# A hybrid decoder trunk: the mixing stage's small inverse, its spreads and its order of work

## The chip, the cores and the metric

The kernel runs on one core of one Trainium2 chip. The metric is the device time of one execution in microseconds (us). The engines are PE (TensorE, the matrix products), DVE (VectorE), ACT (ScalarE), POOL (GpSimd) and SP (SyncE, here only a queue that issues DMA transfers). PEld is the loading of weights into PE, beside its products. A DMA stands in the queue of the engine that issues it, and a queue is worked off in its order.

## What is computed

Two layers, each of a gated feed-forward block, a mixing block and a second feed-forward block, on 512 tokens of width 1024, all in float32. The change touches the mixing block and the normalization ahead of each block. In the mixing block the normalized input is projected to 2560 columns, which three heads of different kind share: sliding-window attention (8 query heads, 2 key heads, window 128, with sinks), RWKV-7 time mixing (4 heads of 64) and a short gated convolution. The outputs are joined and projected back to 1024.

```python
def rms_norm(x, gain):
    y = xf * lax.rsqrt(jnp.mean(xf * xf, axis=-1, keepdims=True) + EPS)
    return y * gain
def sliding_window_sink_attention(qkv, q_gain, k_gain, sinks):
    ...
    scores = einsum('bnqhgd,bnkhd->bnhgqk', qb, kb) * HEAD_DIM ** -0.5
    probs = softmax(concatenate([where(mask, scores, -inf), sink], -1))[..., :-1]
    out = einsum('bnhgqk,bnkhd->bnqhgd', probs, vb)
def rwkv7_time_mix(p, mu, ...):
    p = p + mu * (token_shift(p) - p)
    r, k, v, wd, ad, gd = split(p, ...)
    ...
    def step(S, inp):
        s_kk = einsum('bhvk,bhk->bhv', S, kk_t)
        S = S * w_t - s_kk * (kk_t * a_t) + v_t * k_t
        return S, einsum('bhvk,bhk->bhv', S, r_t)
    y = group_norm(scan(step)) ; y = (y + sum(r * k * r_k) * v) * g
```

## The kernel before

Activations lie with features on the 128 partitions and the 512 tokens along the free axis. A product of a weight tile and an activation tile in float32 is made of three products (`mm3`, L113 to 120): the high part of the weight with the high and the low part of the activation, and the low part of the weight with the high part. They stand in the profile as L118, L119 and L120. The split of a weight tile is a cast on ACT (wH, L130) and a subtraction on DVE (wL, L132), and `load_w` (L277 to 286) brings the raw tile (wraw, two buffers) through SP's queue.

`mix()` (from L577) holds the mixing block. The large projection is a row of 20 tiles of 24 products each, written by the generator `products()` (L668) in the order decay/iclr, k (two), key (kt), value (vr), query (four), r (two), v (two), gate (gd) and convolution (six). Two PSUM banks named "mm" take the tiles in turn, so a tile's first product waits until the tile two before it has left its bank: for r, v and gd by `shifted` (L620), a copy on ACT (L622) and two or more steps on DVE (L627). Beside it three generators run, each in small steps:

- `inverse()` (L800) inverts 64x64 unit triangular blocks (32 of them, two q halves). It takes LT, the masked products of beta and a in B, and moves its 16x16 diagonal blocks through DRAM: two transfers into dl (L809) and sixteen small ones into G (L815). On DVE it then runs 15 elimination steps of two instructions each (elim L822, inv L823; step 7 is followed by a pause). One transfer into di (L828) and sixteen into C (L831) bring the result back, and T and its transpose TT are made on DVE (L837, L838). All 35 transfers of a layer are issued by SP.
- `rwkv()` (L843) makes roots of sums of squares (`roots`, L644) and spreads each over the 64 partitions of its head by products with the identity (`spread_heads`, L660: ps_kk for kk, ps_ks for kt, ps_v for the group norm), then the pairs of chunks (ps_c on PE, masked into B and K on DVE, L924), the bonus (ps_bo), four sets of block transposes (vN with ps_vN, AX with ps_ta, beN, kaN), the corrections of T and TT in two levels (ps_x, X L1012, ps_t, L1023), and the state.
- `attention()` (L1110) works through four blocks of 128 queries: scores (ps_sc, Sc), the softmax (mx, es, the exponentials on ACT in L1150, the division L1178 to 1180), transposes of the probabilities (ps_pt on PE, pmc and pmp on DVE L1167), products with V (ps_av) and a copy of the result into qr (L1190).

Which step stands where is set by a loop with a clock, at the end of `mix()`. Each step of a generator yields two numbers: how far it moves the clock, and how long its successor must wait, which a table `PACE` scales per generator; a group of three large products moves the clock by `STEP`, 0.65. When a step is due, it is written into the program behind the large products so far, and its first matmul is held there (`pe`, L632).

```python
n = min(live, key=ready_.get, default=None)
if n and (ready_[n] <= clock or stuck or not more):
    clock = max(clock, ready_[n])
    lead[0] = latest["large"]
    step = next(live[n], None)
    ...
    clock += step[0]
    ready_[n] = clock + step[1] * PACE[n]
```

Within one engine the order of instructions is fixed when the program is built. The norm ahead of every block spreads the reciprocal root of each half of the tokens over the partitions by two 128x128 products with the identity (`spread`, L258, ps_rstd L264).

Of the kernel before, what the change touches and what calls it, by code (L numbers as in the profile page):

```python
# [17 lines left out]
P = 128  # L18
# [16 lines left out]
PACE = {"rwkv": 1.15, "att": 1.05, "LT": 1.0}  # L35
# [24 lines left out]
def trunk_kernel(ctx, tc, ins, out, layers=L, phases=("ffn1", "mix", "ffn2")):  # L60
# [177 lines left out]
    def norm(l, g, ish, isc, ss):  # L238
# [21 lines left out]
        def spread(sl):  # L260

            r, pt = rstd[sl.start], psum([P, T // 2], "ps_rstd", "r0" if sl.start else "x")
            for b in range(2):
                mm(pt[:, b * P : (b + 1) * P], r[:, b : b + 1].to_broadcast([P, P]), cst("ident"), start=True, stop=True)  # L264
            rstd[sl.start] = pt
# [311 lines left out]
    def mix(l, hn, ss, mp, then, ready):  # L577
# [66 lines left out]
        def roots(srcs, name, bias, scale, low=None):  # L644
# [13 lines left out]
            return r  # L658

        def spread_heads(r, pts):  # L660

            for i, pt in enumerate(pts):
                for b in range(NB):
                    for g in range(2):
                        pe(pt[rows[g], b * P : (b + 1) * P], r[:, i, b, g : g + 1].to_broadcast([P, CH]), cst("ident"), start=True, stop=True)
            return pts

        def products():  # L668
# [108 lines left out]
            done.add("in")  # L777
            while "ya" not in done:
                yield "stuck"
# [4 lines left out]
            for i in range(KD - 2):  # L784
                w = load_w(wo1[l, i, :, :6], 6)
                pt = psmm()
                for k in (4, 5, 0, 1, 2, 3):
# [12 lines left out]
        def inverse():  # L800
# [6 lines left out]
            for q in range(2):  # L807
                dl = dram.tile([P, 2 * NB, CH], F32, name="dl", tag=f"dl{q}", bufs=2)
                nc.sync.dma_start(dl, LT[q].rearrange("p e b t -> p (e b) t"))  # L809
                for c in range(2):  # L810
                    for m in range(NM):
# [3 lines left out]
                        nc.sync.dma_start(G[n : n + 2 * NB], src.rearrange("r n t -> n r t"))  # L815
# [12 lines left out]
            nc.sync.dma_start(di.rearrange("q m n t u -> (q m n) t u"), V_)  # L828
            for q in range(2):
                for m in range(2 * NM):  # L830
                    nc.sync.dma_start(C_[q][m * BASE : (m + 1) * BASE], di[q, m].rearrange("n t u -> t n u"))  # L831
# [11 lines left out]
        def rwkv():  # L843
# [47 lines left out]
            yield 1.0, 6.5  # L891
# [33 lines left out]

            pairs(be, B_, 0, 1)
# [7 lines left out]
            yield 0, 3.2  # L934
            while "r" not in done:
# [9 lines left out]
            yield 1.4, 2.6  # L945
            while "v" not in done:
                yield 0, STEP
# [6 lines left out]
            AX = [U(q, "AX", [P, 2, NB, 2, CH]) for q in range(2)]  # L954
            vN, beN, kaN = ([blocks(S(q, n)) for q in range(2)] for n in ("vN", "beN", "kaN"))
            qs = both()
            pv, pt = banks("ps_vN"), banks("ps_ta")
            for q in qs:
                for b in range(NB):
                    pe(blocks(pv[q])[:, b], v_[q][:, b * P : (b + 1) * P], cst("cen"), start=True, stop=True)  # L960
                turn_(blocks(pt[q]), AR[q][:, 0].rearrange("p c t -> p (c t)"))
            for q in qs:
                nc.scalar.copy(vN[q], blocks(pv[q]))
                for e in range(2):
                    nc.scalar.copy(AX[q][:, e, :, 0], blocks(pt[q])[:, :, rows[e]])
            yield 2.6, 3.4
            qs = both()
            pv, pt = banks("ps_beN"), banks("ps_kaN")
            for q in qs:
                turn_(blocks(pv[q]), be[q])  # L970
                turn_(blocks(pt[q]), ka[q])
            for q in qs:
                nc.scalar.copy(beN[q], blocks(pv[q]))
                nc.scalar.copy(kaN[q], blocks(pt[q]))
            yield 1.8, 3.2

            corners = [(b, e, c) for b in range(NB) for e, c in ((1, 1), (1, 0), (0, 1), (0, 0))]

            def quarters(name, n=1, w=CH):
                return [[psum([P, n, NB, w], name, R[q]) for _ in range(2)] for q in range(2)]  # L980

            def gathered(pts, j):

                return [(slice(0, P), 0, pts[0][:, j])] + [(rows[c], 1, pts[1][rows[1 - c], j]) for c in range(2)]

# [12 lines left out]
            T_, TT = got["T"], got["TT"]  # L998
            X = [S(q, "X", (P, 2, NB, CH)) for q in range(2)]

            def each(q, pts, j, lhs, rhs):
                for b, e, c in corners:
# [492 lines left out]
```

## Time and profile before

| | |
|---|---|
| median of three runs | 1843.88 us (1842.59 to 1846.69) |
| profiled execution | 1847.01 us, of which the span is 1845.0 |
| mixing stages | about 380 to 600 and 1285 to 1505 us |
| DMA, mean over the span | 167 GB/s |

The span runs from the first to the last recorded instruction of the profiled execution; some 2 us lie around it. Rows of a timeline give the start in us from the span's start, the duration, the engine, the line, the operation and output<-inputs, with the idle time before it and what ended it in brackets. A row "PE ps_sc L634 <- ACT qr L1190: 2.3, 1, 2.3" of the waits says that PE, at a product into ps_sc, stood idle for 2.3 us until ACT's step on qr was done. x4 counts neighbouring instructions in one row; a float32 product of the small kind takes several passes and stands as several instructions.

### The profile page before, as it was taken

The numbers are of one execution on the slowest core, as the hardware profiler recorded it, in microseconds if no ns is written. First come the engines' busy times: TensorE is split into PE (matmuls) and PEld (weight loads), VectorE is DVE, ScalarE is ACT, GpSimd is POOL, SyncE is SP. The second block draws the span as 40 slices with busy tenths as digits, with TensorE's granted clock in tenths as the row PEclk, the third lists the DMA queues.
The fourth block names the chain that finished last, engine by engine and source line by source line (L and its number), as shares of the span: only waits on it lengthen the run. The fifth ranks groups of instructions, "written<-read, shape, count | busy, mean of one in ns | idle before, by whom it ended". The sixth has DMA issues, their size and how long they took to land.

```text
span 1845.0 us, 34043 instructions
## 1 busy us (share of the span) xinstructions
PE 1797.7 (97%) x13996; PEld 1634.6 (89%) x13996; DVE 1354.7 (73%) x2185; ACT 837.6 (45%) x1284; POOL 130.7 (7%) x208
## 2 busy tenths in 40 slices
PE   8999999999999999999999999999999999999999
PEld 6889899987778899899999988999867788999998
DVE  6687687876776787678878786878677677874872
ACT  4443255363533554145446524544544445532551
POOL 0101110100000001110100011110000000110000
PEclk8999999999999999999999999999999999999999
DMA  7667876623112476886737688773321125774742
GB/s 312 225 179 237 287 200 198 217 75 99 34 45 91 121 206 188 280 206 198 250 110 197 172 275 233 194 227 123 109 76 39 59 78 158 215 221 139 203 140 69
DMA packets 104284, 308.37 MB, mean 167 GB/s; under 512 B 23360, under 2 KB 24384, under 8 KB 103104
## 3 DMA queue, kind: packets, MB, share of 16 engines
q1 hardware_dynamic: 75904, 203.42, 33.2%
q0 software_dynamic: 28224, 102.77, 22.2%
q8 instruction: 110, 1.80, 0.4%
q14 instruction: 46, 0.38, 0.1%
HBM read 302.74 MB, written 3.41 MB: 166 GB/s over the span
## 4 chain that ended last, share of the span: by engine, by line
PE 73%; DVE 11%; DMA 6%; issue 4%; ACT 4%; POOL 1%; SPq 1%; DVEq 0%; ACTq 0%; POOLq 0%
PE ps_mm L118 11%; PE ps_mm L119 11%; PE ps_mm L120 11%; PE ps_d L414 6%; PE ps_d L416 6%; PE ps_d L415 6%; PE ps_f L415 3%; PE ps_f L416 3%; PE ps_f L414 3%; DVE wL L132 2%; DMA wada<-in_wadaT 2%; PE ps_g L416 2%; ACT wH L130 2%; PE ps_g L415 2%; PE ps_g L414 2%
## 5 line engine op out<-in xcount | busy, mean ns | idle before, releaser
L130 ACT CAST wH<-wraw 128x1024 fp32r<-128x1024 f32 (+2 forms) x292 | 265.8, 917 | 471.6 <-PE ps_mm L119 218.4
L132 DVE TENSOR_TENSOR wL<-wraw,wH 128x1024 fp32r<-128x1024 f32 (+2 forms) x292 | 308.5, 1061 | 123.7 <-ACT wH L130 122.2
L120 PE MATMUL ps_mm<-actH,wL 128*128 128x512 f32 (+1 forms) x784 | 280.7, 358 | 1.3 <-DVE wL L132 1.3
L118 PE MATMUL ps_mm<-actH,wH 128*128 128x512 f32 (+1 forms) x784 | 281.0, 358 | 0.0
L119 PE MATMUL ps_mm<-actL,wH 128*128 128x512 f32 (+1 forms) x784 | 280.5, 358 | 0.0
L118 PE MATMUL ps_mm<-hnH,wH 128*128 128x512 f32 (+1 forms) x760 | 268.1, 360 | 11.0 <-DVE mx L1142 3.3
L119 PE MATMUL ps_mm<-hnL,wH 128*128 128x512 f32 (+1 forms) x760 | 267.1, 353 | 1.1 <-DVE hnL L273 0.9
L120 PE MATMUL ps_mm<-hnH,wL 128*128 128x512 f32 (+1 forms) x760 | 264.9, 351 | 0.6 <-DVE wL L132 0.6
L414 PE MATMUL ps_d<-comH,wH 128*128 128x256 f32 x816 | 226.3, 277 | 0.0
L416 PE MATMUL ps_d<-comH,wL 128*128 128x256 f32 x816 | 226.0, 277 | 0.0
L415 PE MATMUL ps_d<-comL,wH 128*128 128x256 f32 x816 | 225.9, 277 | 0.0
L188 DVE SCALAR_TENSOR_TENSOR wada<-wada,crep 128x1024 f32<-128x1024 f32 x140 | 167.7, 1221 | 47.5 <-DMA wada<-in_wadaT 47.2
L132 DVE TENSOR_TENSOR wL<-sum,wH 128x1024 fp32r<-128x1024 f32 x102 | 125.0, 1225 | 73.6 <-ACT wH L130 73.5
L118 PEld LDWEIGHTS ps_mm<-hnH,wH 128*128 128x128 f32 x760 | 143.5, 192 | 39.0 <-issue 13.8
L120 PEld LDWEIGHTS ps_mm<-actH,wL 128*128 128x128 f32 x784 | 148.7, 190 | 18.9 <-DVE wL L132 2.1
L119 PEld LDWEIGHTS ps_mm<-actL,wH 128*128 128x128 f32 x784 | 148.7, 190 | 16.7
L118 PEld LDWEIGHTS ps_mm<-actH,wH 128*128 128x128 f32 x784 | 148.7, 190 | 16.5
L119 PEld LDWEIGHTS ps_mm<-hnL,wH 128*128 128x128 f32 x760 | 145.9, 192 | 17.4 <-DVE hnL L273 2.2
L120 PEld LDWEIGHTS ps_mm<-hnH,wL 128*128 128x128 f32 x760 | 145.9, 192 | 15.9 <-DVE wL L132 1.4
L414 PEld LDWEIGHTS ps_d<-comH,wH 128*128 128x128 f32 x816 | 158.2, 194 | 0.6 <-ACT s L440 0.6
L415 PEld LDWEIGHTS ps_d<-comL,wH 128*128 128x128 f32 x816 | 158.2, 194 | 0.0
L416 PEld LDWEIGHTS ps_d<-comH,wL 128*128 128x128 f32 x816 | 158.1, 194 | 0.0
(358 smaller groups left out, 3753.0 us busy)
## 6 DMA issues: line engine op xcount, KB each, us to landing
wada<-in_wadaT POOLq DMA_DIRECT2D x128, 512.0 KB, 4.8
wraw<-in_wmi SPq DMA_DIRECT2D x40, 512.0 KB
wraw<-in_w2p SPq DMA_DIRECT2D x36, 512.0 KB
wraw<-in_w1p SPq DMA_DIRECT2D x32, 512.0 KB
wraw<-in_w1o SPq DMA_DIRECT2D x32, 384.0 KB
wraw<-in_w2o SPq DMA_DIRECT2D x32, 384.0 KB
wraw<-in_w1i SPq DMA_DIRECT2D x20, 512.0 KB
wraw<-in_w1o SPq DMA_DIRECT2D x32, 320.0 KB
```

The source lines that it names most:

```text
L118: mm(acc, wH, xH, start=start, stop=False)
L119: mm(acc, wH, xL, start=False, stop=False)
L120: latest["large"] = mm(acc, wL, xH, start=False, stop=stop)
L130: nc.scalar.copy(hi, src)
L132: return nc.vector.tensor_sub(lo, src, hi.bitcast(F32))
L188: stt(w, w, 1.0, crep, ALU.mult, ALU.mult, accum_out=out_)
L414: mm(acc, wH, xH, start=start and i + k == 0, stop=False, skip_group_check=True)
L415: mm(acc, wH, xL, start=False, stop=False, skip_group_check=True)
L416: mm(acc, wL, xH, start=False, stop=k == 3, skip_group_check=True)
```

## The change

1. The clock's table: PACE of rwkv from 1.15 to 1.25, of attention from 1.05 to 1.0, and several yields.
2. The norm's spread is made by transposes instead of products with the identity.
3. `roots` writes each root twice 64 columns wide on ACT into a tile "wide", and `spread_heads` makes one 128x128 transpose of it where two products of 64 columns stood.
4. The inverse's 35 transfers per layer are issued by POOL instead of SP.
5. The transposes of beta (beN) and a (ta) stand ahead of the wait for r; those of key (kaN) come with vN.
6. The corrections of T become a generator of their own, which may begin while v is awaited if T is there.
7. Two output tiles begin with their products of the convolution's halves (k = 4, 5) before attention's last step is awaited.

```diff
-PACE = {"rwkv": 1.15, "att": 1.05, "LT": 1.0}
+PACE = {"rwkv": 1.25, "att": 1.0, "LT": 1.0}
 def spread(sl):
-    mm(pt[:, b * P : (b + 1) * P], r[:, b : b + 1].to_broadcast([P, P]), cst("ident"), start=True, stop=True)
+    mm(pt[:, b * P : (b + 1) * P], r[:, b : b + 1].to_broadcast([P, P]), cst("ident"), start=True, stop=True, is_transpose=True)
 def roots(srcs, name, bias, scale, low=None):
-    return r
+    wide = U(0, "wide", [P, n, NB, 2, CH])
+    for i in range(n):
+        nc.scalar.copy(wide[:, i], r[:, i].unsqueeze(3).to_broadcast([P, NB, 2, CH]))
+    return wide
 def spread_heads(r, pts):
-    for g in range(2):
-        pe(pt[rows[g], b * P : (b + 1) * P], r[:, i, b, g : g + 1].to_broadcast([P, CH]), cst("ident"), start=True, stop=True)
+    pe(pt[:, b * P : (b + 1) * P], r[:, i, b].rearrange("p g z -> p (g z)"), cst("ident"), start=True, stop=True, is_transpose=True)
 def products():
+    begun = []
+    for i in range(2):
+        begun.append((load_w(wo1[l, i, :, :6], 6), psmm()))
+        for k in (4, 5):
+            mm3(begun[i][1], begun[i][0], k, xs[k], ALL, k == 4, False)
+            yield
     while "ya" not in done:
         yield "stuck"
...
 def inverse():
-    nc.sync.dma_start(dl, LT[q].rearrange("p e b t -> p (e b) t"))
+    nc.gpsimd.dma_start(dl, LT[q].rearrange("p e b t -> p (e b) t"))
...
-    nc.sync.dma_start(G[n : n + 2 * NB], src.rearrange("r n t -> n r t"))
+    nc.gpsimd.dma_start(G[n : n + 2 * NB], src.rearrange("r n t -> n r t"))
...
-    nc.sync.dma_start(di.rearrange("q m n t u -> (q m n) t u"), V_)
+    nc.gpsimd.dma_start(di.rearrange("q m n t u -> (q m n) t u"), V_)
...
-    nc.sync.dma_start(C_[q][m * BASE : (m + 1) * BASE], di[q, m].rearrange("n t u -> t n u"))
+    nc.gpsimd.dma_start(C_[q][m * BASE : (m + 1) * BASE], di[q, m].rearrange("n t u -> t n u"))
 def rwkv():
     rn = roots(sq, "rn", None, None, 1e-24)
-    yield 1.0, 6.5
+    yield 1.7, 7.2
...
+    pv, pt = banks("ps_beN"), banks("ps_ta")
+    for q in qs:
+        turn_(blocks(pv[q]), be[q])
+        turn_(blocks(pt[q]), AR[q][:, 0].rearrange("p c t -> p (c t)"))
+    for q in qs:
+        nc.scalar.copy(beN[q], blocks(pv[q]))
+        for e in range(2):
+            nc.scalar.copy(AX[q][:, e, :, 0], blocks(pt[q])[:, :, rows[e]])
+    yield 1.8, 3.4
     while "r" not in done:
         yield 0, STEP
...
+    inv = invert()
     while "v" not in done:
-        yield 0, STEP
+        yield next(inv) if "T" in done else (0, STEP)
...
     while "T" not in done:
         yield 0, STEP
-    for lev in range(2):
...
+    yield from inv
...
-    yield 2.8, 0.4
+    yield 3.4, 1.0
     pv = spread_heads(rs, banks("ps_v"))
 def attention():
-    yield 0.4, 2.0
+    yield 0.4, 3.2
     po = psum([P, 4, P], "ps_av")
...
-    yield 1.9, 1.2
+    yield 1.9, 1.6
```

The rows below are the order of instructions of one engine in layer 1, with the line, the operation, output<-inputs and the shape; numbers behind a name tell buffers apart, and x2 counts neighbours. Lines of the changed kernel lie about ten further down in `inverse()` and fourteen in `attention()`.

First the transfers. SP before, from the weight loads ahead of the inverse (wraw<-in_wmi is a tile of the projection's weights, in_wmo of the output projection's; dl, G, di and C are the inverse's):

```order
L1092 DMA gw<-in_gw 128x256
L284 DMA wraw<-in_wmi 128x1024 x4
L809 DMA dl<-B_4188 1024x1x64
L809 DMA dl<-B_4189 1024x1x64
L815 DMA G<-dl 8x16x16 x16
L284 DMA wraw<-in_wmi 128x1024 x4
L828 DMA di<-inv 128x256
L284 DMA wraw<-in_wmi 128x1024
L831 DMA C<-di 16x8x16 x16
L284 DMA wraw<-in_wmi 128x1024 x2
```

SP in the changed kernel at the same place (gw is the gate's small weight), and POOL there, from attention's first clearing of its scores:

```order
L611 DMA lw<-in_lora 128x256
L284 DMA wraw<-in_wmi 128x1024 x4
L1106 DMA gw<-in_gw 128x256
L284 DMA wraw<-in_wmi 128x1024 x11
L284 DMA wraw<-in_wmo 128x768 x6
```

```order
L1134 MEMSET Sc 128x512 x2
L826 MEMSET inv 128x256
L827 MEMSET inv 128x16
L819 DMA dl<-B_4190 1024x1x64
L819 DMA dl<-B_4191 1024x1x64
L825 DMA G<-dl 8x16x16 x16
L838 DMA di<-inv 128x256
L841 DMA C<-di 16x8x16 x16
```

SP's loads follow one another, and dl, G, di and C stand in POOL's queue behind the clearing of Sc and of the inverse's result.

Second, DVE where the elimination begins (elim and inv are its two instructions, r_4415 and r_4442 are the first tile of r, es and den belong to the softmax of block 0). Before:

```order
L1146 TENSOR_TENSOR es<-par,mx 128x4
L627 SCALAR_TENSOR_TENSOR r_4415<-ps_mm,par,r_4415 128x256
L1146 TENSOR_TENSOR es<-par,mx 128x4
L627 SCALAR_TENSOR_TENSOR r_4415<-ps_mm,par,r_4415 128x255
L822 TENSOR_TENSOR elim<-G,inv 128x15
L939 TENSOR_TENSOR AR_4075<-r_4415,P_3950 128x512
L823 TENSOR_TENSOR inv<-inv,elim 128x15
```

And in the changed kernel:

```order
L1160 TENSOR_TENSOR es<-par,mx 128x4 x2
L132 TENSOR_TENSOR wL<-wraw,wH 128x1024
L832 TENSOR_TENSOR elim<-G,inv 128x15
L833 TENSOR_TENSOR inv<-inv,elim 128x15
L832 TENSOR_TENSOR elim<-G,inv 128x28
...
L832 TENSOR_TENSOR elim<-G,inv 128x63
L1181 TENSOR_TENSOR pmc<-ps_pt,con 128x512
L833 TENSOR_TENSOR inv<-inv,elim 128x7x9
L1192 TENSOR_TENSOR den<-den,es 128x4
L627 SCALAR_TENSOR_TENSOR r_4442<-ps_mm,par,r_4442 128x256
L627 SCALAR_TENSOR_TENSOR r_4442<-ps_mm,par,r_4442 128x255
```

The first tile of r stood ahead of the elimination; now one wL stands there, and r comes behind nine of the elimination's products, with the division of Sc and a pmc ahead of it.

Third, DVE where T is made (B and K are the masks of the pairs, v_4607 and v_4582 the first tile of v). Before:

```order
L1133 COPY_PREDICATED Sc<-con,ps_sc 128x256 x2
L924 TENSOR_TENSOR B_4188<-ps_c,con 128x4x64 x2
L924 TENSOR_TENSOR B_4189<-ps_c,con 128x4x64 x2
L1133 COPY_PREDICATED Sc<-con,ps_sc 128x256 x2
L837 TENSOR_TENSOR T_4599<-C,con 128x512
L1141 TENSOR_REDUCE mx<-Sc 128x4
L838 STREAM_TRANSPOSE TT_4601<-T_4599 128x512
L1142 TENSOR_TENSOR mx<-mx,rq 128x4
L1141 TENSOR_REDUCE mx<-Sc 128x4
L627 SCALAR_TENSOR_TENSOR v_4607<-ps_mm,par,v_4607 128x256
L627 SCALAR_TENSOR_TENSOR v_4607<-ps_mm,par,v_4607 128x255
```

And in the changed kernel:

```order
L833 TENSOR_TENSOR inv<-inv,elim 128x15
L627 SCALAR_TENSOR_TENSOR v_4582<-ps_mm,par,v_4582 128x256
L627 SCALAR_TENSOR_TENSOR v_4582<-ps_mm,par,v_4582 128x255
L934 TENSOR_TENSOR K_4192<-ps_c,con 128x512 x2
L934 TENSOR_TENSOR K_4193<-ps_c,con 128x512 x2
L1147 COPY_PREDICATED Sc<-con,ps_sc 128x256 x2
L847 TENSOR_TENSOR T_4640<-C,con 128x512
L934 TENSOR_TENSOR B_4191<-ps_c,con 128x4x64
L848 STREAM_TRANSPOSE TT_4642<-T_4640 128x512
L934 TENSOR_TENSOR B_4191<-ps_c,con 128x4x64
L934 TENSOR_TENSOR B_4190<-ps_c,con 128x4x64 x2
L1147 COPY_PREDICATED Sc<-con,ps_sc 128x256
```

The first tile of v stood behind the first T; now it stands ahead of the masks of K. The masks of B stood ahead of T; now they stand behind the first one, mixed with TT.

90 lines of the change are left out of this document (43 added, 47 removed).

## The prediction

> **What bounds the kernel now.** I read the page's shares first, then its chain of what ended last.
>
> ```profile
> PE 1797.7 (97%) x13996; PEld 1634.6 (89%) x13996; DVE 1354.7 (73%) x2185; ACT 837.6 (45%) x1284; POOL 130.7 (7%) x208
> ```
> ```profile
> PE 73%; DVE 11%; DMA 6%; issue 4%; ACT 4%; POOL 1%; SPq 1%; DVEq 0%; ACTq 0%; POOLq 0%
> ```
>
> TensorE (PE) is busy 97% of 1845.0 us and carries 73% of the chain. So there are two ways to gain: fewer microseconds of PE work, or fewer of its waits. The change lies in the mixing stages, so next come PE's waits there, layer 1 (380 to 620 us), then layer 2 (1285 to 1525 us); columns: total, times, longest.
>
> ```profile
> PE ps_sc L634 <- ACT qr L1190: 2.3, 1, 2.3
> PE ps_av L634 <- DVE pmc L1167: 2.1, 1, 2.1
> PE ps_mm L118 <- DVE mx L1142: 1.3, 1, 1.3
> ...
> PE ps_pt L634 <- DVE inv L823: 0.7, 1, 0.7
> ```
> ```profile
> PE ps_av L634 <- DVE pmc L1167: 2.1, 1, 2.1
> PE ps_mm L118 <- DVE mx L1142: 2.0, 1, 2.0
> PE ps_sc L634 <- ACT qr L1190: 1.5, 1, 1.5
> ```
>
> The first three make 5.7 and 5.6 us. Where VectorE (DVE) stands behind them shows in the table of windows (length, then PE, weight loads, DVE, ACT, POOL busy with counts, clock, DMA share, GB/s):
>
> ```profile
> 440.00:450.00 10.00, 9.34 (x60) 7.49 (x62) 9.69 (x35) 6.08 (x20) 0.00 (x0) 1.00 0.00 0
> 450.00:460.00 10.00, 7.71 (x89) 4.67 (x83) 6.72 (x16) 2.18 (x4) 0.00 (x0) 0.83 0.52 172
> ```
>
> DVE's average of 73% hides 9.69 of 10 us in the first stretch: whatever goes into DVE's order there is late for everyone behind it.
>
> **Part by part: PE's work.** The spreads of the roots stand in the chain, and PE's timeline shows what transposes cost:
>
> ```profile
> 403.73 1.90 PE ps_kk L634 x32
> ...
> 415.13 1.02 PE ps_ks L634 x16
> ...
> 571.09 1.90 PE ps_v L634 x32
> ```
> ```profile
> 479.99 0.38 PE L120 MATMUL ps_mm<-hnH,wL 128*128 128x512 f32 x1
> 480.20 0.60 PE L634 MATMUL ps_beN<-con,a 128*128 128x128 f32 x4
> 480.64 0.60 PE L634 MATMUL ps_kaN<-con,iP 128*128 128x128 f32 x4
> ```
>
> They hold PE for 1.90, 1.02 and 1.90 us. After the change each is one 128x128 transpose where two matmuls of 64 columns stood: 8, 4 and 8. Four transposes start 480.64 − 480.20 = 0.44 after the four before, 0.11 each, so eight make 0.87 and four 0.44. Saved: 1.03 + 0.58 + 1.03 = **2.6 per layer, 5.3 in all**. The norm's spread is two 128x128 matmuls per half, in ten halves:
>
> ```profile
> 364.41 0.61 PE L264 MATMUL ps_rstd<-con,rstd 128*128 128x128 f32 x4
> 364.78 0.36 PE L118 MATMUL ps_mm<-actH,wH 128*128 128x256 f32 x1
> ```
> From start to start they take 0.37, as x4, twice as many as the code has matmuls; two transposes should take 0.19 to 0.22. Ten times some 0.18 is **1.9**. PE's work thus falls by 7.2.
>
> The rows show the transposes pipelined: the last of four lasts 0.60 − 3 × 0.11 = 0.27. [...] Read as a price it is rival D.
>
> The price of the new spreads is ACT's copies into "wide", of 128x512 like this one:
>
> ```profile
> 403.71 0.58 ACT L711 COPY V<-ps_vt 128x512 f32<-128x512 f32 x1
> ```
>
> Two, one and two of them per layer, 0.58 each. The retuned yield puts nine large products (at 480.20 − 479.99 = 0.21 each, 1.9 us) ahead of ps_kk, so 1.2 us of copies lie beside products; for ps_v six products instead of three. I take 0; without that cover it would be up to 1.2 + 0.6 + 1.2 = 3.0 per layer. The moved transposes of beta and a (16, 1.74 us) are the same work earlier. The two begun output tiles fill PE while attention ends, where the waits above show none to fill: 0, bounds −1 and +1 per layer.
>
> **The waits that go.** SyncE's queue (SP) works in order. Its timeline, then DVE's and ACT's:
>
> ```profile
> 424.07 5.81 SPq L815 DMA_DIRECT2D G<-dl  x16
> 429.98 22.03 SPq L284 DMA_DIRECT2D wraw<-in_wmi  x4
> 454.81 0.33 SPq L828 DMA_DIRECT2D di<-inv  x1
> ...
> 457.50 8.29 SPq L831 DMA_DIRECT2D C<-di  x16
> ```
> ```profile
> 448.47 1.21 DVE L132 TENSOR_TENSOR wL<-wraw,wH 128x1024 fp32r<-128x1024 f32 x1
> ```
> ```profile
> 454.75 1.04 ACT L130 CAST wH<-wraw 128x1024 fp32r<-128x1024 f32 x1 [8.67 <-DMA wraw<-in_wmi]
> 455.70 0.58 ACT L1190 COPY qr<-ps_av 128x512 f32<-128x512 f32 x1
> ```
>
> There are two buffers for raw weights. The four loads begin only behind G, and the last of them could not be issued before the wL of 448.47, deep in the elimination, had read a buffer; ACT's third cast waited 8.67 us for it, the copy of qr stood behind that cast, and PE's scores waited 2.3 (1.5 in layer 2). With the 35 transfers on POOL's queue SP has nothing but loads there, one more wL stands ahead of the elimination, and two casts instead of three stand between r's copy and the copy of qr. This wait ends: **−3.8**. Next, v0's eviction (L627) and the corrections of T:
>
> ```profile
> 464.40 0.69 DVE L837 TENSOR_TENSOR T<-C,con 128x512 f32<-128x512 f32 x1 [0.30 <-DMA C<-di]
> ...
> 466.87 0.86 DVE L627 SCALAR_TENSOR_TENSOR v<-ps_mm,par,v 128x256 f32<-128x256 f32 x2
> ...
> 501.71 1.28 DVE L1023 TENSOR_TENSOR T<-T,ps_t 128x256 f32<-128x256 f32 x3
> ```
>
> v0's pieces stood behind T and kept a bank from the next products (1.3 and 2.0); in the new order they stand ahead of the masks: **−3.3**. The twelve corrections of T and TT stood ahead of the pmc for which ps_av waits 2.1 in each layer; as they may now run while v is awaited, that ends: **−4.2**. Sum 11.3.
>
> **The waits that come.** First, DVE's new order puts r0's eviction behind nine elimination steps. The rows (ACT's first):
>
> ```profile
> 443.52 0.67 ACT L622 ACTIVATE r<-ps_mm,om 128x512 f32<-128x512 f32 x1
> ```
> ```profile
> 439.09 0.17 DVE L822 TENSOR_TENSOR elim<-G,inv 128x15 f32<-128x15 f32 x1
> ...
> 441.01 0.20 DVE L822 TENSOR_TENSOR elim<-G,inv 128x39 f32<-128x39 f32 x1
> 441.24 0.20 DVE L823 TENSOR_TENSOR inv<-inv,elim 128x39 f32<-128x39 f32 x1
> ...
> 445.17 0.48 DVE L627 SCALAR_TENSOR_TENSOR r<-ps_mm,par,r 128x256 f32<-128x256 f32 x1
> ...
> 454.59 0.17 DVE L823 TENSOR_TENSOR inv<-inv,elim 128x15 f32<-128x15 f32 x1
> ```
> ```profile
> 443.18 0.63 PE L634 MATMUL ps_pt<-con,Sc 128*128 128x128 f32 x4
> ...
> 465.51 1.02 PE L634 MATMUL ps_bo<-bonus,con 128*128 128x512 f32 x2
> ```
>
> If the elimination starts at about 439.3 (a wL in the place of r0's pieces), the 18 elimination instructions ahead at 0.23 (441.01 to 441.24) and a little more for the longer ones make 4.4, Sc with its small steps 0.8 and pmc 0.6 (T's size, 0.69 with overlap), r0's two pieces 0.9: r0 is out at some 446.0, with the hops between engines, 0.1 each, 446.5. ACT's part of r0 comes behind the exponentials, as r1's did at 443.52, and is not last. PE is through ps_pt at about 443.0 (443.18 less its wait of 0.7, and 0.44 of transposes), and v0's first product needs r0's bank: 3.5 to 3.7 of waiting against 0.7 before. I take +3.0 a layer, **+6.0**; from 0 (the elimination starts later than r0's turn, or the exponentials finish early) to +9.
>
> Second, POOL's transfers. What one costs on POOL:
>
> ```profile
> L202 POOL DMA_DIRECT2D wada<-in_wadaT x128 | 69.1, 557 | 472.2 <-DVE wada L188 276.5 <-DVE wL L132 109.6 <-ACT hn_t L1311 49.3
> L366 POOL DMA_DIRECT2D sum<-in_w2p x18 | 15.6, 865 | 529.3 <-DMA first<-in_w2p 458.5 <-DMA sum<-in_w2p 26.5 <-DVE actL L499 21.4
> ```
>
> So 0.56 for a plain one and 0.87 for one that adds; SP's are 5.81/16 = 0.36 to 8.29/16 = 0.52. I take the plain 0.53 to 0.56. G: SP's first was at 424.07; I let POOL's two dl be out at 424.4, since LT's last mask has one wL more ahead in DVE's order. Then 2.4 through memory as from di to C (454.81 + 0.33 to 457.50), 16 × 0.53 = 8.5, and 2.75 to land (T started at 464.40, and C's first eight issues ended at 457.50 + 8 × 0.52 = 461.65): 438.1, ahead of 439.3, so 0; bounds 0 and +4 a layer. C: the elimination ends at about 455.8 (454.76 before, and a wL more among its steps); di 0.53, 2.4, 8 × 0.53 = 4.2, 2.75: T starts at 465.7, and TT and the masks of B stand behind it in DVE's order until some 468.3. PE comes to ps_bo, which needs a mask's bank, at about 465.8 (465.51 before, with the 2.3 gone and the 3.0 added): +2.5. The second T (4.2 later, by 470.0) holds v1's eviction until some 473.3, and PE is at vN at 472.4: +1.0. Together +3.5 a layer, **+7.0**; bounds 0 (the masks are out in time) and +14.
>
> [...]
>
> **Sum.** Against the profiled run: 1847.0 − 7.2 − 11.3 + 6.0 + 7.0 = 1841.5. That execution (span 1845.0 and 2.0 around it) lies 3.1 above the median of the runs shown, 1843.9, so the forecast is **1838.4**.
>
> **Rivals.** **A, slower: POOL's issue is the new pace.** If one costs 0.87, G lands at 424.4 + 0.7 + 2.4 + 13.9 + 2.75 = 444.1, 4.8 after the elimination could start, and C's two halves come 2.7 and 5.4 later still, of which the second has some 1.4 left to cost: 4.8 + 2.7 + 1.4 = 8.9 a layer on top, 1841.5 + 17.8 − 3.1 = 1856.2. It decides from where G's slack of 1.2 us is used up by 18 transfers, at 0.60 for one. [...] Against: 128 plain ones at a mean of 0.56 beside a busy DVE.
>
> **B: the old waits go and no new ones come.** 1847.0 − 18.5 − 3.1 = 1825.4. It needs r0 out by 443.0 and C by 463. For it: SP's queue is free and waits of DVE's order are often shorter than a count by hand. Against: the order itself, where r0 stands behind pmc.
>
> **C: it doesn't do what it says.** DVE paces the stretch from 439 to 475, so freed PE time there becomes waiting and old waits change only their names; the norm's 1.9 remains: 1847.0 − 1.9 − 3.1 = 1842.0. For it: the 9.69. Against: 6.72 right behind it, where PE waited for a transfer.
>
> **D: a transpose holds PE for its whole 0.27.** 20 a layer make 5.4 for the 4.8 of the three spreads before, and a norm's two 0.55 for 0.37: 2 × 0.6 + 10 × 0.18 = +3.0 instead of −7.2, 1838.4 + 10.2 = 1848.6. Against: the 0.44 between groups of four. [...]
>
> **How the numbers follow.** The forecast has 0.36, its own range 1833 to 1846; B 0.24, C 0.19, A 0.18, D 0.03. The range for 8 in 10 reaches from B's 1825 with a little below, 1824, to 1852, toward A; beyond lie half of A (0.10) and some of B (0.08). A measurement of this kernel can tell about 0.2%, 3.7 us, from no change. Faster, under 1840.2: B 0.24, two thirds of the forecast 0.25, a little of C: 0.53. Within: a third of the forecast, most of C: 0.25. Slower, over 1847.6: A, D and the rest: 0.22.
>
> **What would show it.** PE's timeline: ps_kk about 0.9 long, ps_ks 0.44; else D. PE's waits: no ps_sc on the qr copy and no ps_av on pmc at 2.1; else C. A product of v0 that waits some 3 us for r0 or for DVE near 443 to 446, and ps_bo or the product behind it for a mask some 2.5: the forecast; neither: B. POOL's issues of G: near 0.55 each the forecast, over 0.60 A. What would make me wrong most easily is the start of the elimination, on which both new waits hang: one us there moves each of them by as much.

## The result, and the profile after

The changed kernel takes 1845.74 us (median of 20 runs, 1842.44 to 1852.19), the kernel before 1846.89 in the 20 runs beside it (1839.89 to 1852.16). The ratio is 0.9998, with a 95% interval from 0.9986 to 1.0009: between 2.6 us faster and 1.7 slower. The forecast, 1838.4, was 5.5 below the runs then known; no gain of that size is there, though the time lies inside the range. Those runs were only three, with a median of 1843.88, 3.0 below the twenty beside the changed kernel.

The profiled execution of the changed kernel took 1849.87 us, 4.1 above its median, so its balance against the profile of before (1847.01) tells where time went and came from, not how the last 4 us arise. First its page: the shares, and the shares of the chain.

```profile
PE 1795.0 (97%) x13856; PEld 1633.5 (88%) x13856; DVE 1353.7 (73%) x2185; ACT 843.0 (46%) x1294; POOL 170.2 (9%) x278
```
```profile
PE 64%; DVE 12%; DMA 9%; issue 7%; ACT 6%; POOL 2%; SPq 0%; POOLq 0%; ACTq 0%; DVEq 0%
```

PE's share of the chain fell from 73% to 64%, and the engines behind its waits took what it lost: work went and waiting came. PE's waits say which, in layer 1 (380 to 620 us):

```profile
PE ps_pt L634 <- DVE Sc L1194: 3.1, 2, 2.1
PE ps_bo L634 <- DVE B L934: 2.7, 1, 2.7
PE ps_mm L118 <- DVE elim L832: 1.9, 1, 1.9
PE ps_gn L634 <- ACT AX L1047: 1.3, 1, 1.3
PE ps_pt L634 <- DVE elim L832: 0.9, 1, 0.9
PE ps_kaN L634 <- DVE bonus L1012: 0.8, 1, 0.8
```

The three waits of before (qr 2.3, pmc 2.1, mx 1.3) are all gone from this list, and six others lead it, 10.7 us together. Layer 2 has the same, with 2.2 at ps_bo and without the 0.8 at ps_kaN. Now the two mixing stages whole, from PE's first product on the normalized input to the first sum of squares of the next norm; columns as in the tables of windows above. Before, then after:

```profile
368.14:595.80 227.66, 218.61 (x2240) 177.82 (x2239) 159.39 (x378) 106.69 (x224) 1.80 (x4) 0.99 0.22 67
1275.34:1503.55 228.21, 219.18 (x2241) 178.31 (x2240) 159.52 (x378) 106.56 (x224) 1.80 (x4) 0.99 0.23 66
```
```profile
369.69:598.54 228.85, 216.35 (x2179) 176.66 (x2178) 158.78 (x378) 109.62 (x228) 21.31 (x39) 0.99 0.22 66
1277.60:1507.40 229.80, 218.07 (x2179) 178.19 (x2178) 158.86 (x378) 109.56 (x228) 21.29 (x39) 0.98 0.22 66
```

Each stage is split in three: PE's listed waits; what the half clock took (the sum over 4-us windows of one less the granted clock, times the length); and the rest, PE's work at full clock.

| us, layer 1 / layer 2 | before | after | difference |
|---|---|---|---|
| work | 217.1 / 217.6 | 213.0 / 213.2 | −4.0 / −4.4 |
| waits | 8.9 / 8.9 | 12.4 / 11.5 | +3.5 / +2.6 |
| half clock | 1.7 / 1.7 | 3.4 / 5.1 | +1.7 / +3.4 |
| stage | 227.7 / 228.2 | 228.9 / 229.8 | +1.2 / +1.6 |

The mixing stages are 2.8 us longer, the other stages 0.3. 8.4 us of PE's work went; 6.1 of waiting and 5.1 of half clock ate it. The norms' spreads are 2.3 us shorter, most of it outside the mixing stages; it does not show in the length of the other stages, which varies by 11 us over the sixteen profiles of this case (1379.8 to 1390.7) although no edit but the spreads touches them.

PE's timeline shows the spreads, each with the product behind it:

```profile
406.88 1.04 PE L634 MATMUL ps_kk<-con,wide 128*128 128x128 f32 x8
407.68 0.46 PE L118 MATMUL ps_mm<-hnH,wH 128*128 128x512 f32 x1
...
415.13 0.60 PE L634 MATMUL ps_ks<-con,wide 128*128 128x128 f32 x4
415.49 0.46 PE L118 MATMUL ps_mm<-hnH,wH 128*128 128x512 f32 x1
...
601.43 0.38 PE L264 MATMUL ps_rstd<-con,rstd 128*128 128x128 f32 x2
601.57 0.36 PE L118 MATMUL ps_mm<-yrH,wH 128*128 128x256 f32 x1
```

From start to start ps_kk, ps_ks and a half of a norm hold PE for 0.80, 0.36 and 0.14 us, against 1.89, 1.03 and 0.37 before; ps_v takes 0.79 (576.33 − 575.54) for 1.90. That is 2.9 a layer and 0.23 in each of the ten halves of a norm. Now the first new wait, with what PE runs behind it, and the clock there:

```profile
445.54 0.63 PE L634 MATMUL ps_pt<-con,Sc 128*128 128x128 f32 x4 [0.93 <-DVE elim L832]
...
448.03 0.65 PE L118 MATMUL ps_mm<-hnH,wH 128*128 128x512 f32 x1 [1.86 <-DVE elim L832]
...
471.54 3.30 PE L634 MATMUL ps_bo<-bonus,con 128*128 128x512 f32 x4 [2.71 <-DVE B L934]
```
```profile
448.00:452.00 4.00, 3.97 (x11) 3.23 (x12) 4.00 (x14) 0.00 (x0) 0.00 (x0) 0.57 0.00 0
471.50:473.50 2.00, 1.96 (x3) 0.97 (x4) 0.67 (x2) 0.00 (x0) 0.47 (x1) 0.64 0.22 20
473.50:475.50 2.00, 2.00 (x5) 1.02 (x4) 0.53 (x1) 0.00 (x0) 0.00 (x0) 0.51 0.00 0
```

Behind each of the two stalls PE runs at half its clock for some 3.4 us (granted 0.50 from 448.17 to 451.58 and from 472.06 to 475.47): a product takes 0.65 at 448.03 where 0.46 stands in the rows before. That is 1.7 us lost on top of the stall. A stall does not always bring it. The division of block 2 keeps PE waiting 2.14 us in both layers, and only layer 2 shows half clock there. The rows are windows of 3.41 us, counted from where the other half-clock stretches of this trace begin; two of layer 1 come first, then two of layer 2:

```profile
509.61:513.02 3.41, 1.93 (x68) 1.40 (x66) 3.41 (x8) 0.00 (x0) 0.00 (x0) 1.00 0.35 115
513.02:516.43 3.41, 2.75 (x15) 2.52 (x16) 3.28 (x8) 0.83 (x1) 0.00 (x0) 1.00 0.00 0
1417.55:1420.96 3.41, 1.27 (x12) 1.19 (x9) 3.34 (x8) 0.14 (x1) 0.00 (x0) 1.00 0.24 90
1420.96:1424.37 3.41, 3.41 (x10) 2.69 (x9) 3.35 (x7) 0.69 (x1) 0.00 (x0) 0.50 0.00 0
```

In layer 1 the stall falls across two windows, which leave PE idle for 1.48 and 0.66 us, and the clock stays full, also in the window behind them. In layer 2 it falls into one, idle for 2.14, and the next window runs at half clock. So it is in all sixteen traces, whose half-clock stretches all lie on such a grid. Of the full-clock windows behind the first 60 us in which PE was idle for 2.0 us or more, all 56 were followed by half clock; of those with less than 1.4, 1 of 8090; between the two, 18 of 80.

In the changed kernel 2.13 to 2.71 us of idling were enough for half clock when they fell into one window.

### The profile page after: what moved, and what is told of

It is laid out like the page before. It is cut to its first block, busy times and chain, and to the rows that moved or that the text cites. A ratio compares the mean times of both kernels' runs of the same rounds, so it can differ in the third digit from the quotient of the medians.

```text
span 1848.1 us, 33783 instructions
## 1 busy us (share of the span) xinstructions
PE 1795.0 (97%) x13856; PEld 1633.5 (88%) x13856; DVE 1353.7 (73%) x2185; ACT 843.0 (46%) x1294; POOL 170.2 (9%) x278
## 3 DMA queue, kind: packets, MB, share of 16 engines
HBM read 302.74 MB, written 3.41 MB: 166 GB/s over the span
## 4 chain that ended last, share of the span: by engine, by line
PE 64%; DVE 12%; DMA 9%; issue 7%; ACT 6%; POOL 2%; SPq 0%; POOLq 0%; ACTq 0%; DVEq 0%
PE ps_mm L118 9%; PE ps_mm L119 8%; PE ps_mm L120 8%; PE ps_d L414 6%; PE ps_d L415 6%; PE ps_d L416 6%; DMA wada<-in_wadaT 4%; PE ps_f L415 3%; PE ps_f L414 3%; PE ps_f L416 3%; DVE wL L132 3%; ACT wH L130 2%; DVE wada L188 2%; PE ps_g L416 2%; PE ps_g L415 2%
## 5 line engine op out<-in xcount | busy, mean ns | idle before, releaser
L416 PE MATMUL ps_d<-comH,wL 128*128 128x256 f32 x816 | 226.5, 278 | 0.0
```

The source lines that it names most:

```text
L416: mm(acc, wL, xH, start=False, stop=k == 3, skip_group_check=True)
```

## The experiments

All were timed beside the kernel before; a ratio is to that kernel. The theory after this result: work did go as forecast, and the transfers on POOL's queue (late T, late masks, late v) and r0's late eviction put waits with half-clock stretches in its place. The rivals: that DVE paces the stretch whatever is moved, that half clock alone is the loss, and that the retuned order itself is worse.

**The parts by themselves.** The spreads (parts 2 and 3) alone on the kernel before; and POOL's queue (part 4) alone, the four transfer lines of `inverse()` changed from `nc.sync` to `nc.gpsimd`. The edit of the first is the diff's own lines of `spread`, `roots` and `spread_heads`.

> The kernel before with the new spreads alone (the norm's and the heads' roots as transposes, with the wide copies), no other part. Theory S (PE's work and PE's stalls add up, and a stall of some 2 us costs a stretch at half clock besides): each mixing stage 2.6 us shorter than before's 227.7 and 228.2, the norms 1.9 in all, total -7 us, ratio about 0.996. Rival C (VectorE paces the stretch, so PE work that is saved becomes waiting): only the norms' 1.9, ratio about 0.999, and the waits in PE's list grow by the 2.6.

Measured: 0.996 [0.9944, 0.9976], 1839.54 us.

> The kernel before with the inverse's 35 transfers a layer on POOL's queue, no other part. By the order r0's eviction falls behind ten elimination steps and T stands ahead of half of B's masks. Theory S: the wait of the scores for qr (2.3 and 1.5) and its stretch at half clock (1.7) go; a wait of 3 to 4 for r0 and one of 2 to 3 at ps_bo come, each with 1.7 us lost to the clock: +4 a layer, +8 in all, ratio about 1.004. Rival P (what counts is that SP is free for the weights): the scores' wait and its clock loss go and little comes, -7, ratio 0.996.

Measured: 1.009 [1.0064, 1.0115], 1862.11 us, about 16 us slower where I had expected some 8. PE's waits of layer 1 in these two, the spreads first:

```profile
PE ps_mm L118 <- DVE den L1180: 4.5, 1, 4.5
```
```profile
PE ps_pt L634 <- DVE Sc L1180: 3.9, 1, 3.9
PE ps_mm L118 <- DVE elim L822: 3.8, 1, 3.8
```

The spreads gain 7 us even though v0's bank is now waited for 4.5 us, behind a T that waits for C. The queue costs some 16 us in the old order; the whole change comes out even, so its other parts together win about that much.

**The masks behind T.** Three edits of the changed kernel ask whether the wait at ps_bo and its half clock are the loss: the first T held behind the masks of B; nine products with zero weights ahead of ps_bo, which add nothing to the sums; and each T held behind the masks and its half of v.

```diff
+while "masks" not in got:
+    yield 0, STEP
+m = tt(T4, C_[q]..., msk, ALU.mult)
+if q == 0:
+    tc.add_manual_dep(m.ins, got["masks"].ins.name, ORDER, reason="T stands behind the masks")
```


> The changed kernel with one dependency of order more: on VectorE the first T stands behind all four masks of B. PE's order is unchanged. Theory S: the wait of ps_bo (2.7 and 2.2) goes and with it a stretch at half clock worth 1.7; T comes no earlier, so the second T still holds v1's eviction and ps_vN or the convolution's products may wait 1 to 2 there: -2 to -3.5 a layer, ratio to before about 0.997. Rival M (the late T is what counts, wherever PE meets it): the same wait turns up at ps_vN, the stage keeps its length within 0.5 us, ratio 0.9998.

Measured: 1.0001 [0.9986, 1.0017], 1847.42 us. The wait at ps_bo is gone and another of the same size stands at vN (2.7 in layer 1, 2.3 in layer 2):

```profile
PE ps_vN L634 <- DVE v L627: 2.7, 1, 2.7
```

```diff
+acc, xH = latest["acc"]
+for _ in range(9):
+    last = pe(acc, zeroR[:, :1].to_broadcast([P, P]), xH, start=False, stop=False)
+lead[0] = last
 pb = sums(bo, "ps_bo", qs)
```


> The changed kernel with nine products of zero weights (nothing is added to the sums) ahead of ps_bo, where PE otherwise stands idle for 2.7 and 2.2 us; nine take 1.94 us. Nothing of what PE waits for comes earlier. Theory S, its clock part: PE keeps the full clock behind ps_bo, the stage is 1.7 us shorter in each layer although PE does more, about -3.4 us against the changed kernel, ratio to before about 0.998. Rival (only the wait counts, the slow stretch has another cause): no change, or longer by up to 0.2 a layer; ratio 0.9998.

Measured: 1.003 [1.0016, 1.0043], 1852.24 us. PE's timeline, and the clock right behind:

```profile
471.87 1.98 PE L637 MATMUL ps_bo<-bonus,con 128*128 128x512 f32 x4 [1.55 <-DVE B L937]
...
479.70 0.66 PE L637 MATMUL ps_kaN<-con,iP 128*128 128x128 f32 x4 [1.73 <-DVE bonus L1019]
```
```profile
472.00:474.00 2.00, 2.00 (x6) 1.02 (x7) 1.34 (x4) 0.00 (x0) 0.00 (x0) 1.00 0.06 6
474.00:476.00 2.00, 2.00 (x11) 1.76 (x10) 2.00 (x6) 0.00 (x0) 0.00 (x0) 1.00 0.00 0
```

In layer 1 the fill keeps the clock at 1.00 (0.64 and 0.51 without it), so the stall is what halves it there. But kaN now waits 1.73 for the bonus, which stands on DVE behind the second T and v1, where it waited 0.8 before: part of what the clock gives is waited for a little later. By the balance above, layer 1's stage has no half clock left and is 226.5 long, 2.4 shorter than in the changed kernel; layer 2's has 6.8 of it and is 235.2, with new stalls of 1.8 at ps_vN and ps_kaN. Filling one stall does not settle the clock, and the kernel as a whole is no faster for it. What half clock alone costs the kernel this run cannot tell, as it did not remove it.

The third edit, shown against the first:

```diff
-while "masks" not in got:
+while "v" not in done or "masks" not in got:
     yield 0, STEP
-if q == 0:
-    tc.add_manual_dep(m.ins, got["masks"].ins.name, ORDER, reason="T stands behind the masks")
+for n in (f"v{q}", "masks"):
+    tc.add_manual_dep(m.ins, got[n].ins.name, ORDER, reason="T stands behind what PE waits for")
```


> The changed kernel with order dependencies on VectorE: each T stands behind B's masks and behind the eviction of its half of v. POOL's queue and its late C stay. Theory Q (C lands late, and this costs only because T stands in VectorE's in-order queue ahead of the masks and of v's evictions): the waits of ps_bo (2.7, 2.2) and ps_kaN (0.8) go, the stretch at half clock there (1.7) too; T is first needed at ps_x some 10 us later, so nothing new comes: -4 to -5 a layer, -9, ratio to before about 0.995. Rival K (the arrival of C itself paces the stage): the wait reappears at ps_x, ratio 0.9998.

Measured: 0.997 [0.9955, 0.9985], 1839.73 us. In layer 1, 1.7 is left at vN and 0.6 at kaN; in layer 2, 0.6 at kaN. So DVE's queue, blocked by a T that waits for its transfer, is part of the loss.

> The kernel before with the new spreads and with each T behind B's masks and its half of v; transfers stay on SP, the clock's table and all else as before. Theory Q: against the spreads alone (0.996) the wait of v's product for the eviction behind T (4.5, 4.7) and its stretch at half clock (1.7) go: -6 a layer, ratio to before about 0.9895. Rival K: the wait reappears at ps_x or ps_bo, ratio 0.996.

This is the same order of T on the kernel before with the spreads alone, SP issuing. Measured: 0.9944 [0.9926, 0.9961], 1836.31 us. The 4.5 of the spreads alone is gone, but the division behind T now keeps PE waiting 2.0 in layer 1 and 3.7 in layer 2, and the expected size did not come; against the spreads alone (0.996) the intervals overlap, so that it gains is not shown.

**r0.** First the elimination's first step held behind DVE's steps on r0; then that together with T behind masks and v; then instead the first exponentials of block 0 held behind ACT's copy of r0 (the softmax also waits for it in the clock's loop):

```diff
+tc.add_manual_dep(m.ins, got["r0"].ins.name, ORDER, reason="the elimination stands behind r0")
```
```diff
-act(es, es, AF.Exp)
+m = act(es, es, AF.Exp)
+if b == 0 and g == 0:
+    tc.add_manual_dep(m.ins, got["r0a"].ins.name, ORDER, reason="the exponentials stand behind r0")
```


> The changed kernel with one dependency of order: the elimination starts behind r0's eviction, as it did before. Theory Q: the waits at ps_pt and at v0's first product (0.9 + 1.9) shrink to about 0.7 and the first stretch at half clock (1.7) goes, -3.8 a layer; the elimination ends 1 to 2 later, and C with it, which ps_bo pays: net -2 to -3 a layer, ratio to before about 0.997. Rival K (the chain elimination, di, C, T paces the stage, PE's stalls ahead of it are free): all that is won is lost at ps_bo, ratio 0.9998 or above.

Measured: 1.0017 [0.9999, 1.0036], 1847.69 us. The wait that it was to remove stays:

```profile
PE ps_mm L118 <- DVE elim L836: 1.9, 1, 1.9
```


> The changed kernel with both: elimination behind r0, and each T behind the masks and v. Theory Q: both gains add, -4.5 and -3.8 a layer, -16 in all, ratio to before about 0.991. Rival K: no better than either alone, ratio 0.997 or above.

Measured: 1.0005 [0.9993, 1.0017], 1846.77 us: the same 1.9, and a new 4.0 at ps_pt for the division's den. So the elimination's place in DVE's order is not what makes r0 late. ACT's timeline shows r0's copy in the kernel before, in the changed kernel, and with the exponentials held:

```profile
437.42 0.69 ACT L622 ACTIVATE r<-ps_mm,om 128x512 f32<-128x512 f32 x1 [5.63 <-PE ps_mm L120]
```
```profile
440.32 1.28 ACT L1161 ACT_TABLE_LOAD   x1
...
445.64 1.24 ACT L622 ACTIVATE r<-ps_mm,om 128x512 f32<-128x512 f32 x2
```
```profile
438.62 0.68 ACT L622 ACTIVATE r<-ps_mm,om 128x512 f32<-128x512 f32 x1
```

In the changed kernel the copy stands behind the load of the exponential's table and the exponentials (L1161, L1164) and runs 8.2 us later than before (6.7 counted from the stage's start), though it needs none of them. DVE's two steps on r0 come later still, behind the pmc of block 0, which needs the same exponentials:

```profile
446.21 0.69 DVE L1181 TENSOR_TENSOR pmc<-ps_pt,con 128x512 f32<-128x512 f32 x1 [0.16 <-PE ps_pt L634]
...
447.02 0.87 DVE L627 SCALAR_TENSOR_TENSOR r<-ps_mm,par,r 128x256 f32<-128x256 f32 x2
```

> The changed kernel with one order dependency on ScalarE: r0's copy (L622) stands ahead of block 0's eight exponentials, as before the change; nothing else is forced. Theory A (r0 is late because its copy stands behind the exponentials on ScalarE; putting the elimination behind r0 on VectorE alone left the wait of 1.9 in place): v0's first product waits no more (1.9 gone), ps_pt's 0.9 grows by up to the copy's 0.6, and the stretch at half clock behind it (1.7, where it falls) goes: -1.3 to -3 a layer, ratio to before about 0.997. Rival D (VectorE's elimination ahead of r0 is what makes it late): the wait of 1.9 stays, ratio 0.9998.

Measured: 0.9959 [0.9942, 0.9976], 1839.88 us. The 1.9 and the 0.9 are gone. The edit names ACT alone, but r0's steps moved on DVE too, from behind pmc to behind the first of the elimination's instructions:

```profile
439.98 0.48 DVE L627 SCALAR_TENSOR_TENSOR r<-ps_mm,par,r 128x256 f32<-128x256 f32 x1
```

Which of the two moves was needed no run separates. The whole stretch moves up until PE meets the next thing that is late:

```profile
PE ps_vN L634 <- DVE v L627: 4.8, 1, 4.8
```

**The queue.** The changed kernel with its four transfer lines on SP again:

```diff
-nc.gpsimd.dma_start(G[n : n + 2 * NB], ...)
+nc.sync.dma_start(G[n : n + 2 * NB], ...)
```


> The changed kernel with the inverse's transfers back on SP; PE's order is the same, on VectorE B's masks come ahead of T by themselves. Theory Q (POOL's queue makes C late: 0.6 for an issue and 3.9 through DRAM, against 0.36 to 0.52 and 2.4 on SP): T starts 4 to 5 earlier, ps_bo waits under 1 instead of 2.7, -3 a layer, ratio to before about 0.996. Rival P (SP's loads of weights are held up again behind the transfers): the scores wait for a cast some 2 in each layer, ratio 0.9998 or above.

Measured: 0.9938 [0.9918, 0.9957], 1834.36 us; the changed kernel has 0.9998, so POOL's queue costs it about 0.6%, 11 us. Of the 14.4 us between the two profiled executions, 7.8 lie in the mixing stages (4.3 of waits, 3.4 of half clock); the other stages, which the edit does not touch, account for the rest. POOL's issues in the changed kernel, then the same on SP (the first column behind the start is the time over all issues of the row):

```profile
426.18 9.44 POOL L825 DMA_DIRECT2D G<-dl  x16 [0.22 <-issue]
...
458.58 0.60 POOL L838 DMA_DIRECT2D di<-inv  x1 [22.95 <-issue]
463.13 3.16 POOL L841 DMA_DIRECT2D C<-di  x6 [3.96 <-issue]
```
```profile
460.20 0.33 SPq L838 DMA_DIRECT2D di<-inv  x1
462.49 8.16 SPq L841 DMA_DIRECT2D C<-di  x16
```

POOL's di ends its issue at 459.18 and C begins at 463.13: 3.95 us for the way through memory, against 1.96 here and 2.36 in the kernel before on SP. The queue by itself does not explain it. With the exponentials held, POOL takes 1.97 for the same step; one thing that differs is what the DMA engines move in the first 2 us of it (the last two columns), 225 GB/s in the changed kernel and 109 there:

```profile
459.70 3.16 POOL L843 DMA_DIRECT2D C<-di  x6 [1.97 <-issue]
```
```profile
459.18:461.18 2.00, 2.00 (x11) 1.43 (x8) 2.00 (x4) 0.58 (x1) 0.00 (x0) 1.00 0.59 225
457.73:459.73 2.00, 2.00 (x15) 1.54 (x12) 1.53 (x5) 0.00 (x0) 0.03 (x2) 1.00 0.29 109
```

So it is on POOL in all ten traces with its queue: 1.97 to 2.22 us beside at most 115 GB/s, 3.66 to 4.33 beside 225 or more, as in the changed kernel, where SP's queue moves 0.52 MB, one load of weights, between 458 and 464. On SP it is 1.53 to 2.36 beside at most 92 (two traces), but with heavier traffic 1.9 in two traces and 2.7 to 4.2 in two others. That the load makes the step long is argued from this, not tested. One issue of C is 0.52 on POOL (of G 0.59) and 0.51 on SP. What DVE waits for follows, changed kernel first:

```profile
469.20 0.69 DVE L847 TENSOR_TENSOR T<-C,con 128x512 f32<-128x512 f32 x1 [5.10 <-DMA C<-di]
470.77 1.05 DVE L934 TENSOR_TENSOR B<-ps_c,con 128x256 f32<-128x256 f32 x3
474.97 0.69 DVE L847 TENSOR_TENSOR T<-C,con 128x512 f32<-128x512 f32 x1 [2.80 <-DMA C<-di]
```
```profile
467.69 0.69 DVE L847 TENSOR_TENSOR T<-C,con 128x512 f32<-128x512 f32 x1 [2.19 <-DMA C<-di]
```

On SP the masks of B come ahead of T by themselves, and the wait at ps_bo is gone. The wait for qr, which POOL's queue was to remove, did not come back: in this order SP's loads are early enough anyway. Where the DMA engines move at most 115 GB/s beside it, the way from one issue to the next that depends on it is about 2 us by both queues: 1.97 to 2.22 on POOL, 1.53 to 2.36 on SP.

**Together.** The exponentials behind r0's copy and both T behind the masks and v1, on POOL and on SP.

> The changed kernel, transfers on POOL, with r0's copy ahead of the exponentials and both T's behind B's masks and the second half of v. Theories A and Q together: the waits of v0's product (1.9), ps_bo (2.7, 2.2) and ps_kaN (0.8) go with their stretches at half clock; ps_pt for the blocks behind (3.1) and ps_gn (1.3) stay: -5 to -7 a layer, ratio to before 0.993 to 0.994. Rival K (the chain through C paces): ps_x or ps_pt waits instead, ratio 0.997 as with T behind v alone.

Measured: 0.995 [0.9933, 0.9967], 1837.92 us, not clear of r0's order alone (0.9959).

> The same with the transfers on SP; VectorE's and PE's orders are the same but for a few neighbours in the elimination. It tells what the queue itself is worth once a late T holds up nobody. Theory Q: nothing, the same ratio as on POOL within 0.001. Rival P (SP's loads are held up): slower than on POOL by 0.002 or more, with a wait of the scores or of products for a weight's cast.

Measured: **0.9891 [0.987, 0.9911], 1826.77 us**, 20 us faster than the kernel before, the best of all. I had expected both alike. One thing that differs: the second T, and behind it the divisions, wait for C longer on POOL (PE's waits at ps_pt are 6.4 and 5.4 us in layer 1, 6.9 and 4.5 in layer 2). The order that hides T does not hide the whole queue. That is not all of it: of the 9.5 us between these two profiled executions the mixing stages hold 3.7, and the other 5.8 lie in stages that no edit here touches, for which I have no cause. With SP one large wait is left, at ps_pt for the divisions.

**The division.** Block 2's divisions ahead of the corrections of the first level: on the changed kernel, and on the best.

```diff
+while lev == 0 and "div21" not in got:
+    yield 0, STEP
...
+if lev == 0:
+    tc.add_manual_dep(m.ins, got["div21"].ins.name, ORDER, reason="corrections behind the division")
```


> The changed kernel with block 2's two divisions (L1194) ordered ahead of the first level's corrections of T and TT on VectorE (which the planner answers by moving the second ps_x and the level behind it back by some products). Theory V (the wait of 3.1 at ps_pt is the corrections' and the convolution's place in VectorE's order): ps_pt waits under 0.5 there, -2.6 a layer and up to 1.7 more where a stretch at half clock goes: ratio to before 0.996 to 0.997. Rival N (as before the change, the wait only takes another name, ps_av on pmc or ps_w on TT, some 2 a layer): ratio 0.999 to 1.000.

Measured: 1.002 [1.0001, 1.0039], 1849.78 us. The wait for the division gives way to one of 2.7 us at the scores (ps_sc, for DVE's step on Sc).

> The kernel of e12 with the same. Theory V: its waits at ps_pt for blocks 2 (3.1 of the 5.4 and 4.5) go, -2.6 a layer, ratio to before about 0.986. Rival N: no better than e12, 0.989, or worse where ps_w comes late.

Measured: 0.9925 [0.9903, 0.9946], 1834.02 us, no better than without it (0.9891; the two intervals just touch), with the same 2.7. In the stretch around the division DVE has hardly a gap, as its busy time in the changed kernel shows (third after the length):

```profile
500.00:520.00 20.00, 16.92 (x239) 13.12 (x233) 18.50 (x46) 6.40 (x21) 0.00 (x0) 1.00 0.10 34
```

18.5 of 20 us: what was moved ahead in these two runs made something else late by about as much.

## Why the prediction was wrong, step by step

- **PE's work, −7.2: right, a little small.** The three spreads gave 2.9 a layer for the forecast 2.6, the norms 2.3 for 1.9. PE's work in the mixing stages fell by 1.1 to 1.5 a layer more, 1.0 of it at ps_av (7.7 us before, 6.6 after, from start to start), whose products no longer stand in pieces around the wait for pmc. The copies into "wide" cost PE nothing that shows. Rival D is out: eight transposes hold PE for 0.80.
- **The waits that go, −11.3: the three names went, the third term failed.** The step that failed was "as they may now run while v is awaited, that ends: −4.2". They do not run there: in the order as built, the corrections' wait for v ends before T is there (made at 469.20 and 474.97). Written without the early start of part 6, the kernel builds to the same program, so that start does nothing. The wait took other names: 3.1 for the division and 1.3 for AX's copy. DVE is busy for 18.5 of 20 us there, so what rival C said of the stretch from 439 to 475 holds of this one, and the two runs with the division first bear it out. Rival B, the old waits gone and none new, is out: 12.4 and 11.5 us of waits stand where 8.9 stood.
- **r0, +6.0: time right, cause wrong.** Forecast 3.0 a layer over the old 0.7; measured 0.9 + 1.9, so 2.1 over it. Counted from the stage's start, which is 1.55 later than before, r0 is out at 446.3 for the 446.0 to 446.5 forecast. The 0.1 for a hop between engines in that sum was an estimate that no run shows; in the profile of before, PE begins ps_sc 0.05 after ACT's copy of qr ends (455.70 + 0.58 to 456.33). The failed step is that nine elimination steps hold it. With the elimination behind r0, PE still lost 0.4 + 1.9. The chain that holds r0 is that of block 0's softmax: exponentials, division, ps_pt, pmc, and only then r0's steps on DVE. That ACT's part "is not last" is so in the changed kernel (445.64 against 447.02), but it is hardly earlier, and the runs that removed the loss had r0 ahead of that chain on both engines. That the count came so near was in part luck, as it put the elimination in the place of that chain.
- **POOL's transfers, +7.0: place and size right, working wrong.** ps_bo waits 2.7 and 2.2, kaN 0.8 in layer 1, for 3.5 forecast. T started at 469.20, not 465.7: its way through memory took 3.95, beside a load of weights, and not the 2.4 carried over from SP, and the elimination ended 2 us later. That the size came out is luck: PE too came to ps_bo 3.0 later than forecast (471.54 − 2.71 = 468.83 for 465.8). G cost 0, as said: the elimination starts at 441.48, behind a wL, with G landed. POOL issues at 0.59 (9.44/16) where rival A needs 0.87, and G was in time, so A is out. As to the whole step, the runs with SP say that the queue costs the changed kernel some 11 us, of which the profiles find 7.8 in the mixing stages, nearly half of that as half clock.
- **No term for half clock: the second step that failed.** It took 5.1 us more in the two mixing stages than before. The profile of before had it: the stretch of 450 to 460 that the prediction quotes shows a clock of 0.83, and I used that row for DVE's load alone.

```profile
456.30:458.30 2.00, 1.97 (x9) 1.17 (x9) 0.75 (x1) 0.01 (x1) 0.00 (x0) 0.57 0.12 19
458.30:460.30 2.00, 2.00 (x35) 1.26 (x39) 0.78 (x2) 0.63 (x2) 0.00 (x0) 0.58 0.75 256
```

These are the two windows behind the old wait for qr. In the mixing stages, then, waits and half clock come to +11.2 where the forecast had −11.3 + 13.0 = +1.7, and work to −8.4 where it had −5.3. That difference, +6.4, is most of the 8.4 by which the profiled execution missed (+2.9 for −5.5); the rest is about the norms' 1.9, which do not show in the other stages. Between the medians of twenty runs the miss is 4.3 (−1.15 for −5.5).

Not settled: the clock's table and yields (part 1), the earlier transposes (part 5) and the begun output tiles (part 7) were not run by themselves. On SP the rest of the change is worth 0.9938 and the spreads alone 0.996; the intervals overlap, so whether those parts gain anything is open. Open too is why the other stages' length differs between profiles.

## What to carry to other kernels

Here a T that waited 5.10 us for its transfer held up the masks and evictions behind it in DVE's order, and PE stood idle for 2.7 us at ps_bo; so put evictions first, and look at each engine that takes part in one: r0's copy on ACT stood behind the exponentials and its steps on DVE behind a product that hangs on them, and moving the elimination alone gained nothing (1.0017). Where PE stood idle for 2.0 us or more in one window of 3.41, half clock followed in all 56 cases here, at 1.7 us each: count it too, and check what would wait next if the stall were filled. Do not carry a small transfer's way through memory from one order of work to another: on POOL it took 1.97 to 2.22 us beside at most 115 GB/s and 3.66 to 4.33 beside 225 or more. The freed queue of SP was worth nothing in the changed order, which meets its loads in time anyway.

## What had not been expected of the hardware

The way from di's issue to C's on POOL's queue is about 2 us beside at most 115 GB/s of traffic and 3.7 to 4.3 beside 225 or more. A group of transposes costs PE 0.10 each (0.80 for eight). Half clock followed a stall of 2.14 us in layer 2 and not the one of 2.14 at the same place in layer 1; it came behind all 56 windows of 3.41 us with 2.0 or more of idling, and behind 1 of 8090 with less than 1.4.
